# A list scheduler gets a second transfer regime and a table of 215 pairs of priority shifts

## The chip, the cores and the metric

The kernel runs on all eight cores of one Trainium2 chip. Each core computes one of eight batch elements with the same program; the cores exchange nothing. The metric is device time in microseconds (us) of the slowest core. In some runs one die shows a clearly lower TensorE clock and takes longer (the slow state: in one slow run cores 4 to 7 had mean clocks of 0.833 to 0.854, cores 0 to 3 had 0.987 to 0.994); such runs are left out of the medians and ratios below. "Faster" and "slower" mean a ratio more than 2% away from 1.

## The reference, cut to what matters

One layer of a decoder, for 16 meta tokens and 2048 tokens of width 1024:

```python
h = layer_norm(concat([meta, x]))                       # embed
proj = h @ w_in                                         # latents, keys, values, gates
o_mla = causal_block_attention(q_mla, k_mla, v_mla)     # first attention, 8 heads
o_fox = causal_block_attention(fq, fk, fv, cum_logf)    # second attention, 8 heads
merged = g_mla * (o_mla @ w_branch_mla) + g_fox * (o_fox @ w_branch_fox)
h = layer_norm(DN_ALPHA * h + merged @ w_out)           # merge
f = (silu(causal_depthwise_conv(h @ w_up_gate)) * (h @ w_up_val)) @ w_down   # MLP
out = layer_norm(DN_ALPHA * h + f)[16:]
```

## The kernel before

The program is not written in the order in which it runs. A `Recorder` notes some 11,500 items (matmuls, activations, vector operations, transfers) with their dependences, tiles and priorities. Its `order()` then plays a list scheduler through, with a small model of every engine: whenever a modelled engine is free, it takes the ready item of the smallest priority number. The result is a fixed order for each engine, a slot for each tile and, for copies that two engines can do, the engine. On the chip nothing of this is decided again: each engine executes its list strictly in order, and waits on a semaphore where an input is not there. The traces of before show the order: the eight cores ran one and the same sequence of 1,674 instructions on VectorE, 1,362 on ScalarE and 258 on GpSimd, and the six cores whose traces hold every matmul one and the same sequence of 8,316 on TensorE.

```python
class Recorder:
    RES = {"pe": 165.0, "act": 100.0, "dve": 72.0, "pool": 45.0, "sp": 0.0}
    SEM = {"pe": 145.0, "act": 98.0, "dve": 107.0, "pool": 144.0, "sp": 120.0}
    ...
    COLD = 10.0
    RATE = 250.0
    LAND = {"sp": 2000.0, "pool": 2300.0}
    ...
    def _prio(self, e, prio):
        b = prio if prio is not None else self.base.get(e, self.base.get("", 0.0))
        return b * 1e6 + len(self.items)
    ...
    def order(self):
        ...
            if it.dma is not None:
                ks = ["%s%d" % (it.dma, i) for i in range(self.nkeys.get(it.dma, 2))]
                k = min(ks, key=lambda q: keyend.get(q, 0.0))
                st = max(now, keyend.get(k, 0.0))
                bus[0] = max(st + (1450.0 if e == "sp" else 1900.0), bus[0]) + it.bytes / self.RATE + 20.0
                end = bus[0] + self.LAND[e]
                keyend[k] = end
                ...
            else:
                ...
                if e == "pe" and st < 1e3 * self.COLD:
                    dur *= 2
        ...
        self.span = max(freet.values())
```

`self.span` is what I call the scheduler's own **forecast**. A modelled transfer takes 1.45 us to start, then its bytes at 250 bytes per ns on one shared bus, then 2.0 us until its data may be used. *Transposes* (`K.flip`) carry normalised rows and latents into transposed layout, and TensorE multiplies what they deliver. *Loads* bring rows and weight chunks. *Paced casts* copy weights from float32 to bfloat16 in DRAM; they are issued from GpSimd, one at a time, after an activation that the model chose.

```python
        for c in range(8):                       # rank 1: 32 casts for the merge
            for a in (0, 1536):
                for r in range(0, 128, CUT):
                    K.paced(1, "pool", scr_c[c, r:r + CUT, a:a + 1536], d_c[c, r:r + CUT, a:a + 1536], key="pc")
        for j in AHEAD:                          # rank 4: 88 casts for the MLP
            for a in (0, 1024):
                for r in range(0, 128, CUT):
                    K.paced(4, "pool", scr_u[j, r:r + CUT, a:a + 1024], d_u[j, r:r + CUT, a:a + 1024], key="pc")
```

The softmax here doesn't subtract the row's maximum and nothing guards it: scores larger than these inputs give would overflow.

Of the kernel before, what the change touches and what calls it, by code (L numbers as in the profile page):

```python
# [12 lines left out]
class _Op:  # L13
    __slots__ = ("eng", "stream", "pos", "fn", "waits", "clock", "signal", "sigval", "dma")

    def __init__(self, eng, stream, pos, fn, dma):
        self.eng = eng
        self.stream = stream
        self.pos = pos
        self.fn = fn  # L20
        self.waits = []
        self.clock = None
        self.signal = dma
        self.sigval = 0
        self.dma = dma
# [305 lines left out]
class Recorder:  # L331
# [8 lines left out]
    COLD = 10.0  # L340
    RATE = 250.0
    LAND = {"sp": 2000.0, "pool": 2300.0}

    def __init__(self, S):
        self.S = S
        self.items = []
        self.state = {}
        self.nt = 0
        self.base = {}
        self.line = None  # L350
        self.nkeys = {"sp": 16, "pool": 8, "pc": 8, "out": 4, "flip": 8}
        self.pools = []
        self.slow = []

    def slots(self, name, slots, quota=None):
        p = Slots(self, name, slots, quota)
        for s in slots:
            p.keys.update(self.S._keys(s))
        for k in p.keys:
            st = self.state.get(k)  # L360
            if st is not None:
                if st[0] is not None:
                    p.opened.add(st[0])
                p.opened.update(st[1])
        self.pools.append(p)
        return p
# [19 lines left out]
    def _item(self, alts, prio):  # L386
        it = Item()
        it.idx = len(self.items)
        it.alts = alts
        it.tiles = []  # L390
        it.preds = set()
        it.succ = []
        it.dma = None
        it.bytes = 0
        it.done = False
        it.ready = 0.0
        it.end = 0.0
        it.eng = None
        it.prio = prio
        it.key = None  # L400
        it.after = None
        it.tick = False
        it.rank = None
        self.items.append(it)
        return it

# [145 lines left out]

    def _prio(self, e, prio):
        b = prio if prio is not None else self.base.get(e, self.base.get("", 0.0))
        return b * 1e6 + len(self.items)

    def copy(self, out, in_, engs=("act", "dve"), prio=None):
        alts = []
# [31 lines left out]
    def order(self):  # L590
# [17 lines left out]
        bus = [0.0]  # L608
# [55 lines left out]
        def can(it, now):  # L664
            got = {}
            for t in it.tiles:
                if t.slot is None:
                    p = t.pool
                    m = got.get(id(p), 0)
                    ml = got.get((id(p), t.line), 0)  # L670
                    if p.turn.get(t.line, 0) + ml != t.seq:
                        return p, None
                    if p.used.get(t.cls, 0) + m >= p.quota.get(t.cls, 99):
                        return p, None
                    if len(p.free) <= m:
                        return p, None
                    w = p.free[0][0] if m == 0 else sorted(p.free)[m][0]
                    if w > now:
                        return p, w
                    got[id(p)] = m + 1  # L680
                    got[(id(p), t.line)] = ml + 1
            return None, None
# [9 lines left out]
        while ev:  # L692
            now, _, e = heapq.heappop(ev)
            if freet[e] > now + 1e-6:
                continue
            pq = pend[e]
            aq = avail[e]
            while pq and pq[0][0] <= now + 1e-6:
                _, _, it = heapq.heappop(pq)
                if not it.done:  # L700
                    heapq.heappush(aq, (it.prio[e], it.idx, it))
            pick = None
            later = []
            while aq:
                pr, ix, it = heapq.heappop(aq)
                if it.done:
                    continue
                p, when = can(it, now)
                if p is None and it.dma is not None:
                    w = min(keyend.get("%s%d" % (it.dma, i), 0.0) for i in range(self.nkeys.get(it.dma, 2)))  # L710
                    if w > now:
                        p, when = it, w
                if p is not None:
                    if when is None:
                        lst = blocked.setdefault(id(p), [])
                        if it not in lst:
                            lst.append(it)
                    else:
                        later.append((it, when))
                    continue  # L720
                pick = it
                break
            for it, when in later:
                heapq.heappush(pq, (when, it.idx, it))
                wake(when, e)
            if pick is None:
                if pq:
                    wake(max(pq[0][0], now), e) if pq[0][0] > now else None
                continue
            it = pick  # L730
            for t in it.tiles:
                if t.slot is None:
                    p = t.pool
                    _, t.slot = heapq.heappop(p.free)
                    p.used[t.cls] = p.used.get(t.cls, 0) + 1
                    p.turn[t.line] = p.turn.get(t.line, 0) + 1
                    for b in blocked.pop(id(p), []):
                        for (e2, *_r) in b.alts:
                            heapq.heappush(pend[e2], (max(b.ready, now), b.idx, b))
                            wake(max(now, freet[e2]), e2)  # L740
            alt = next(a for a in it.alts if a[0] == e)
            st = now
            dur = alt[4]
            if it.dma is not None:
                ks = ["%s%d" % (it.dma, i) for i in range(self.nkeys.get(it.dma, 2))]
                k = min(ks, key=lambda q: keyend.get(q, 0.0))
                st = max(now, keyend.get(k, 0.0))
                bus[0] = max(st + (1450.0 if e == "sp" else 1900.0), bus[0]) + it.bytes / self.RATE + 20.0
                end = bus[0] + self.LAND[e]
                keyend[k] = end  # L750
                it.key = k
                freet[e] = st + dur
                out.append((it, alt))
                finish(it, "sp", st, end)
            else:
                if e in shape:
                    rw = self.rows(alt[1], alt[2], alt[3])
                    if rw != shape[e]:
                        st = max(st, freet[e] + self.SHIFT)
                        shape[e] = rw  # L760
                if e == "pool" and alt[1] == "tensor_tensor" and port[0] < st < port[1]:
                    dur = max(dur, port[1] + 367.0 - st)
                if e == "dve" and self.twin(alt[1], alt[3]):
                    port = (st, st + dur + 72.0)
                if e == "pe" and st < 1e3 * self.COLD:
                    dur *= 2
                freet[e] = st + dur
                out.append((it, alt))
                finish(it, e, st, st + dur)
                if it.tick and slow and st >= tick and bus[0] <= st + dur + 2100.0 + 1e3 * self.QUIET:  # L770
                    q = next((q for q in slow if q.left == 1), None)
                    if q is not None:
                        slow.remove(q)
                        tick = st + 1e3 * self.GAP
                        q.after = it
                        q.left = 0
                        q.ready = max(q.ready, st + dur + self.RES[e] + self.SEM["pool"])
                        push(q)
            ndone += 1
            wake(freet[e], e)  # L780
# [6 lines left out]
    def replay(self):  # L787
        S = self.S

        def res(v):  # L790
            return v.at(v.t.slot) if isinstance(v, View) else v

        for it, (e, name, args, kw, _d) in self.done:
# [7 lines left out]
            else:  # L801
                it.op = S.op(e, name, *[res(a) for a in args], **kw)

D = 1024
SEQ = 2048
NMETA = 16
# [37 lines left out]
def build_program():  # L844
    nc = bass.Bass("TRN2", target_bir_lowering=False)
    dt_in = lambda n, s: nc.dram_tensor(n, s, F32, kind="ExternalInput").ap()
    xm = dt_in("xm", [L, D])
    lnp = dt_in("lnp", [6, D])
    d_lat = dt_in("w_lat", [128, 8 * 512])
# [16 lines left out]
    d_kt = dt_in("c_kt", [128, NT * 48])  # L866
    out = nc.dram_tensor("out", [SEQ, D], F32, kind="ExternalOutput").ap()
    scr_h2 = nc.dram_tensor("scr_h2", [LP, D], F32, kind="Internal").ap()
    scr_c = nc.dram_tensor("scr_c", [8, 128, 3072], BF16, kind="Internal").ap()
# [858 lines left out]
```

## Time and profile before

| | kernel before |
|---|---|
| time, median of 3 runs | 1097.69 us (1096.46 to 1097.96) |
| spans of the eight cores in the profiled run | 1089.0 to 1095.9 us |
| TensorE busy | 97% of the span |

A core's time divides into stages that the trace marks by the shapes of its matmuls. Medians over the eight cores: the first 65-column matmul (first attention) starts at 70.9 us, the first 64-row matmul (second attention) at 277.3 us, the first 386-column matmul (MLP) at 607.1 us, and the last matmul ends 12.3 us before the end.

The page of the slowest core: the span, the first engine line (busy us and share) and the chain of work that ended last, by engine.

```profile
span 1095.9 us, 25665 instructions; the slowest of 8 cores (1089.0 to 1095.9 us)
...
PE 1061.2 (97%) x8230; PEld 602.7 (55%) x8316; DVE 744.7 (68%) x1674; ACT 619.9 (57%) x1362; POOL 178.9 (16%) x258
...
PE 88%; DMA 3%; issue 2%; ACT 2%; DVE 2%; POOL 1%; SPq 0%; DVEq 0%; POOLq 0%; ACTq 0%
```

TensorE (PE) is the bound, and transfers are hardly on the chain. The waits of TensorE on core 1 from 55 to 165 us, the stretch where transposes feed it (what it waited for: us in total, times, longest):

```profile
PE PS L187 <- ACT SB L187: 2.2, 6, 1.0
PE PS L187 <- DVE SB L187: 1.2, 2, 0.9
PE PS L187 <- DMA SB<-SB: 0.4, 2, 0.2
```

`DMA SB<-SB` is a transpose: the only transfers from on-chip memory to on-chip memory.

Windows of core 0 (busy us of each engine in the stretch, then PEclk, the granted TensorE clock as a share of full speed, then DMA share and GB/s):

```profile
78.00:82.00 4.00, 4.00 (x54) 2.79 (x54) 4.00 (x15) 2.49 (x9) 1.54 (x2) 1.00 0.71 106
82.00:86.00 4.00, 3.96 (x30) 2.06 (x28) 3.79 (x11) 3.88 (x10) 2.53 (x3) 1.00 0.66 154
```

### The profile page before, as it was taken

Reading aid. Unit: us, or ns where it says so; the run is one execution under the profiler, and the core shown is the slowest. Engines: PE = TensorE matmul, PEld = TensorE weight load, DVE = VectorE, ACT = ScalarE, POOL = GpSimd, SP = SyncE. Lnnn points to the kernel's source line nnn. Section 1 sums busy time; section 2 is a strip of 40 time slices with the busy share of each in tenths; the row PEclk is TensorE's granted clock in tenths of the full one; section 3 lists DMA queues with packets and bytes.
Section 4 is the critical chain, followed back from the end, with each engine's and each line's share of the span. In section 5 each row is a group of like instructions: output and inputs, shape, how many; then the busy total and the mean of one; then the engine's idle time right before and its main releaser. Section 6 shows DMA issues by size and latency. Waiting matters only on the chain.

```text
span 1095.9 us, 25665 instructions; the slowest of 8 cores (1089.0 to 1095.9 us)
## 1 busy us (share of the span) xinstructions
PE 1061.2 (97%) x8230; PEld 602.7 (55%) x8316; DVE 744.7 (68%) x1674; ACT 619.9 (57%) x1362; POOL 178.9 (16%) x258
## 2 busy tenths in 40 slices
PE   9999889999999999999999999999999999999995
PEld 6655556667454555565555566554456664444443
DVE  3899866764566676766668887656576765667754
ACT  5789879999778888887873254431034431023300
POOL 5434221121111220302111111101100000110010
PEclk9999999999999999999999999999999999999998
DMA  8858865754677797886989386962242232234301
GB/s 174 206 106 137 146 76 78 137 81 62 156 160 174 123 226 215 148 250 128 226 213 281 98 239 158 257 162 96 99 154 97 97 105 73 112 127 151 107 20 58
DMA packets 86867, 156.54 MB, mean 143 GB/s; under 512 B 39073, under 2 KB 43121, under 8 KB 86737
## 3 DMA queue, kind: packets, MB, share of 16 engines
q1 hardware_dynamic: 70066, 123.78, 38.4%
q0 software_dynamic: 16672, 31.11, 21.3%
q8 instruction: 72, 1.18, 0.5%
q14 instruction: 57, 0.47, 0.2%
HBM read 160.38 MB, written 34.67 MB: 178 GB/s over the span
## 4 chain that ended last, share of the span: by engine, by line
PE 88%; DMA 3%; issue 2%; ACT 2%; DVE 2%; POOL 1%; SPq 0%; DVEq 0%; POOLq 0%; ACTq 0%
PE PS L187 88%; ACT SB L187 2%; DVE SB L187 2%; DMA SB<-SB 2%; DMA SB<-scr_c 1%; POOL SB L187 1%; SPq L190 0%; ACT L187 0%; DVEq L226 0%; POOLq L226 0%; DVEq L245 0%; POOL scr_c L190 0%; POOL SB L190 0%; ACTq L245 0%; SPq L245 0%
## 5 line engine op out<-in xcount | busy, mean ns | idle before, releaser
L187 PE MATMUL PS<-SB 128*128 128x65 bf16 (+11 forms) x8230 | 1061.2, 291 | 22.5 <-DVE SB L187 6.7
L187 PEld LDWEIGHTS PS<-SB 128*128 128x128 bf16 (+2 forms) x8316 | 602.7, 98 | 480.7 <-issue 88.4
L187 ACT ACTIVATE SB<-PS,SB 128x384 bf16<-128x384 f32 (+9 forms) x611 | 315.3, 582 | 250.8 <-PE PS L187 243.9
L187 ACT ACTIVATE SB<-PS 128x384 bf16<-128x384 f32 (+11 forms) x547 | 215.3, 537 | 28.5 <-PE PS L187 24.5
L187 DVE SCALAR_TENSOR_TENSOR SB<-SB 128x1024 f32<-128x1024 f32 (+7 forms) x188 | 177.4, 948 | 14.6 <-POOL SB L187 7.1
L187 ACT ACTIVATE SB<-SB 128x384 f32<-128x384 f32 (+4 forms) x153 | 97.7, 645 | 141.4 <-DVE SB L187 141.1
L187 DVE SCALAR_TENSOR_TENSOR SB<-SB,PS 128x512 f32<-128x512 f32 (+3 forms) x146 | 90.2, 620 | 118.2 <-PE PS L187 93.7
L187 DVE SCALAR_TENSOR_TENSOR SB<-PS,SB 128x384 f32<-128x384 f32 (+1 forms) x220 | 141.0, 642 | 31.9 <-ACT SB L187 23.1
L187 POOL TENSOR_TENSOR SB<-SB 128x1 f32<-128x1 f32 (+1 forms) x67 | 81.8, 1222 | 434.1 <-DVE SB L187 433.6
L187 DVE TENSOR_TENSOR SB<-PS,SB 128x384 bf16<-128x384 f32 (+10 forms) x229 | 108.6, 480 | 61.1 <-ACT SB L187 53.7
L187 DVE TENSOR_TENSOR SB<-SB 128x128 bf16<-128x128 bf16 (+7 forms) x353 | 84.7, 268 | 31.2 <-ACT SB L187 23.7
L190 POOL DMA_DIRECT2D scr_u<-w_u x88 | 44.5, 506 | 266.9 <-ACT SB L187 261.7
L187 DVE CAST SB<-PS 128x512 bf16<-128x512 f32 (+5 forms) x85 | 50.6, 599 | 23.1 <-PE PS L187 18.5
L187 DVE BATCH_NORM_STATS2 SB<-SB 128x6 f32<-128x512 f32 (+1 forms) x85 | 56.9, 675 | 4.6
L187 DVE COPY SB<-SB 32x384 bf16<-32x384 bf16 (+2 forms) x80 | 19.7, 260 | 14.1 <-PE PS L187 12.5
L190 POOL DMA_DIRECT2D scr_c<-w_c x32 | 16.6, 520 | 64.6 <-ACT SB L187 62.7
L187 DVE COPY SB<-PS 128x2 f32<-128x2 f32 (+9 forms) x66 | 19.7, 306 | 8.1 <-PE PS L187 7.7
L190 POOL DMA_DIRECT2D SB<-w_dn x22 | 11.9, 541 | 78.4 <-ACT SB L187 78.4
L187 DVE TENSOR_SCALAR SB<-SB 128x1 f32<-128x1 f32 (+2 forms) x68 | 10.3, 152 | 18.7 <-ACT SB L187 15.9
L187 DVE RECIPROCAL SB<-PS 128x3 f32<-128x3 f32 (+3 forms) x84 | 14.1, 173 | 12.6 <-PE PS L187 11.2
L187 DVE TENSOR_SCALAR SB<-PS,SB 128x128 bf16<-128x128 f32 (+1 forms) x21 | 9.5, 461 | 1.4 <-POOL SB L187 1.0
L187 DVE BATCH_NORM_AGGREGATE SB<-SB 128x2 f32<-128x12 f32 (+2 forms) x43 | 8.6, 203 | 2.4
(20 smaller groups left out, 38.9 us busy)
## 6 DMA issues: line engine op xcount, KB each, us to landing
SB<-scr_u SPq DMA_DIRECT2D x66, 512.0 KB, 3.9
SB<-scr_c SPq DMA_DIRECT2D x80, 384.0 KB, 5.3
SB<-xm SPq DMA_DIRECT2D x31, 512.0 KB, 6.8
scr_u<-w_u POOLq DMA_DIRECT2D x88, 128.0 KB, 4.0
scr_h<-SB SPq DMA_DIRECT2D x16, 512.0 KB, 4.9
SB<-scr_h SPq DMA_DIRECT2D x16, 512.0 KB, 3.5
out<-SB SPq DMA_DIRECT2D x15, 512.0 KB, 2.6
scr_c<-w_c POOLq DMA_DIRECT2D x32, 192.0 KB, 4.2
```

The source lines that it names most:

```text
L187: return self._add(eng, lambda e: getattr(e, name)(*args, **kw), rd, wr)
L190: return self._add(eng, lambda e: e.dma_start(out=out, in_=in_, **kw), [in_], [out], dma_key=key, after=after)
```

## The change

The intent is a better static order, in two parts. The model of transfers gets a second regime: a transfer that starts after 56 us moves 290 bytes per ns and may be used 1.0 us (1.2 us from GpSimd) after its last byte, not 2.0 (2.3). And the program is split into parts, a new one wherever the recorder's stage name changes; each part shifts the priority of its items by a number from a table, one for TensorE and one for the other engines. No arithmetic and no transfer is added or removed.

```diff
+    LATER = 56.0
+    RATE2 = 290.0
+    LAND2 = {"sp": 1000.0, "pool": 1200.0}
...
     def _prio(self, e, prio):
         b = prio if prio is not None else self.base.get(e, self.base.get("", 0.0))
-        return b * 1e6 + len(self.items)
+        k = self.part + (self.line != self.of or self.part < 0)
+        return b * 1e6 + len(self.items) + (RAISED[k][e != "pe"] if k < len(RAISED) else 0)
...
-                bus[0] = max(st + (1450.0 if e == "sp" else 1900.0), bus[0]) + it.bytes / self.RATE + 20.0
-                end = bus[0] + self.LAND[e]
+                late = st >= 1e3 * self.LATER
+                bus[0] = max(st + (1450.0 if e == "sp" else 1900.0), bus[0]) + it.bytes / (self.RATE2 if late else self.RATE) + 20.0
+                end = bus[0] + (self.LAND2 if late else self.LAND)[e]
...
+RAISED = ((-98184, -12242), (90515, -18772), (174186, -48968), ... some 210 more pairs
```

## The prediction

> **What bounds the kernel now.** The page: span 1095.9 us on core 2, TensorE busy 97%. Cores range from 1089.0 to 1095.9 us (view of the cores), clock 0.99. [...] the chain of waits repeats every 10.79 us, 50 matmuls of 512 columns, 216 ns each. All matmuls of core 1 at that rate (my estimate) take 1026 us, 22 of them the 200 filler matmuls at the start. With the table of windows, time minus that work is:
> - 0 to 55 us: 10 us plus most of the filler; first loads bound this (DMA share 0.81).
> - 55 to 164 us: 11 us on core 1, 20 us on core 2. VectorE is 97% busy from 55 to 110 us. On core 2 TensorE waits 5.3 us (waits view, DMA SB<-SB) for DMA transposes that took 6 to 8 us; one slice has clock 0.94.
> - 164 to 274 us: 6 us; ScalarE is 96 to 100% busy (exponentials of the first attention).
> - 274 to 301 us: 5 us, the turn to the second attention.
> - 301 to 575 us: 20 us, but TensorE is 99% "busy": short 65-column matmuls (76 ns each in the groups[...]). Order hardly touches that.
> - 575 to 1069 us: 1 us.[...]
> - tail: 12 us of LayerNorm and store.

> **What the change does.** It adds and removes no operation. It alters the static order: each engine's queue, the slots of the rings, whether ScalarE or VectorE takes a flexible copy, when paced weight casts start. By my reading the 215 parts run to about the end of the merge; the MLP is one late part and stays. Base priorities in the first attention differ by 5,000 a tile and the shifts are tens of thousands: strong reordering. In the second attention bases differ by 100,000 or more: less.

> The modelled transfer after 56 us becomes shorter: a lone 512 KB load 4.3 us, old 5.6; the trace has 3.9. That is better. For a full transpose it becomes worse: 3.2 us, old 4.4, trace median 5.4. An order computed with it can place consumers of transposes too early, and TensorE, in order, waits.

> **Cost.** Addressable is the loss between 27 and 301 us (25 to 35 us); VectorE, then ScalarE are over 95% busy there, so only overlap of the two stages helps. I expect a third: 10 us, plus 2 us from the second attention, less 2 us for transposes later than modelled. All of it is on the critical path: TensorE has no slack afterwards, so the MLP starts earlier by what is gained, unchanged in length. Net 10 us.

> **Prediction: 1087 us, 8 in 10 between 1076 and 1098.** Faster by over 2% (under 1075.7): 0.09. Within 2%: 0.88. Slower by over 2%: 0.03.

> **What would show it.** The first up matmul (386 columns), at 611 us on core 2, comes 6 to 14 us earlier; from there to the end the time stays within 2 us. Loss in 55 to 301 us falls by about 10 us; VectorE and ScalarE totals stay within 10 us. TensorE's waits on DMA SB<-SB remain or grow. Loss in 301 to 575 us stays 17 to 20 us. The tail stays 12 us.

> **What would make it wrong.** The shifts were fitted to a model, and the chip differs: waits on transposes could eat the gain (1095 or more). Or the first 55 us, with the filler, is shortened too, or core 2's loss to clock and transposes vanishes: then 1075.

The chain of waits of which it speaks is that of the MLP. The trace shows the rates themselves: on core 1 of before, after the first 30 us, the median from the start of one matmul to the next is 216 ns for 512 columns, 162 ns for 384 and 29 ns for 65. With these medians for every shape (an estimate, without 8 float32 matmuls for which there is none) the matmuls of core 1 take 1020 us, and the losses by window are 10.4, 10.8 (19.9 on core 2), 6.4, 5.1, 20.6 and 1.6 us, so the list above stands. 10 + 2 - 2 = 10 us, and 1097 less 10 is 1087.

## More of the kernel before

Core 7 from 300 to 600 us, the second attention, hardly waits:

```profile
PE PS L187 <- DVE SB L187: 0.2, 1, 0.2
PE PS L187 <- ACT SB L187: 0.2, 1, 0.2
```

## The result, and the profile after

| | before | after |
|---|---|---|
| time, median of the fast runs | 1097.1 us (4 runs) | 1117.65 us (3 runs, 1116.07 to 1119.36; with the one slow run, 1259.5, the median is 1118.51) |
| ratio of fast runs | | 1.0182 (95% interval 1.0164 to 1.0199) |
| spans of the cores | 1089.0 to 1095.9 us | 1098.9 to 1117.8 us |

A ratio is the mean time of one kernel's fast runs over the mean of the other's fast runs of the same rounds, so it is not quite the ratio of the medians. The change made the kernel 1.8% slower. By the 2% rule that counts as "same", but the interval is far from 1. The page, as shown of before:

```profile
span 1117.8 us, 25623 instructions; the slowest of 8 cores (1098.9 to 1117.8 us)
...
PE 1066.6 (95%) x8230; PEld 601.7 (54%) x8316; DVE 746.3 (67%) x1674; ACT 619.3 (55%) x1362; POOL 177.9 (16%) x258
...
PE 78%; DMA 8%; ACT 4%; issue 4%; DVE 3%; SPq 1%; POOL 1%; DVEq 0%; POOLq 0%; ACTq 0%
```

The work of every engine is the same to within 6 us. What changed is the chain: TensorE falls from 88% to 78% of it and transfers rise from 3% to 8%. Also, the eight cores, which differed by 7 us, now differ by 19 us, although all run the same list. The waits of TensorE on core 1, 55 to 170 us:

```profile
PE PS L187 <- DMA SB<-SB: 9.4, 7, 3.5
PE PS L187 <- ACT SB L187: 2.1, 6, 0.8
PE PS L187 <- DVE SB L187: 1.5, 2, 1.3
PE PS L187 <- issue: 0.2, 1, 0.2
```

The 0.4 us of waiting for transposes have become 9.4 us. Core 1 shows this most clearly; over all eight cores these waits were 0 to 5.3 us before (mean 1.5) and 5.3 to 10.1 after (mean 6.9). The transposes themselves hardly slowed down: those issued between 55 and 166 us took 4.7 us before and 5.2 after, means over the cores. Core 7 from 300 to 600 us, where there was next to no wait before:

```profile
PE PS L187 <- ACT SB L187: 4.9, 4, 3.7
PE PS L187 <- DVE SB L187: 3.6, 3, 2.1
```

On the mean of the cores TensorE waited 0.7 us in this stretch before and 5.4 after. What VectorE (DVE) waited for tells more. In the same window and on the same core it waited for loads of input rows (`xm`); before there is no such line:

```profile
DVE SB L187 <- DMA SB<-xm: 9.9, 6, 3.7
```

These loads did not take longer. Their lines in the DMA view of core 7, the same window, before and then after (the last number is the median from issue to landing):

```profile
SB<-xm SPq DMA_DIRECT2D x16, 512.0 KB, 6.5
SB<-xm SPq DMA_DIRECT2D x13, 512.0 KB, 6.7
```

So the changed order leaves them less time. On the mean of the cores VectorE waited 8.4 us for row loads (before 0.2), and ScalarE 2.0 us for transposes (before 0).

One of TensorE's waits for a transpose, in its timeline on core 0 (start, length, instructions, and in brackets the idle time before them with what ended it):

```profile
73.83 3.71 PE L187 MATMUL PS<-SB 128*128 128x384 bf16 x20
81.86 2.63 PE L187 MATMUL PS<-SB 128*128 128x512 bf16 x16 [4.33 <-DMA SB<-SB]
```

And the windows of core 0 around it, with those of a second wait that ends at 666 us:

```profile
78.00:82.00 4.00, 0.14 (x1) 0.10 (x1) 1.26 (x4) 1.11 (x3) 0.70 (x1) 1.00 0.81 186
82.00:86.00 4.00, 4.00 (x23) 2.53 (x23) 2.45 (x7) 2.47 (x6) 0.00 (x0) 0.57 0.19 71
...
662.00:666.00 4.00, 0.25 (x2) 0.00 (x0) 3.67 (x10) 1.08 (x2) 0.00 (x0) 0.97 0.41 144
666.00:670.00 4.00, 3.55 (x12) 1.91 (x13) 2.98 (x10) 0.52 (x1) 1.62 (x3) 0.50 0.40 47
```

The second wait is named after VectorE, which had itself just waited for a load (`lnp`, the LayerNorm parameters):

```profile
662.22 0.48 DVE L187 SCALAR_TENSOR_TENSOR SB<-SB 128x256 f32<-128x256 f32 x1 [4.22 <-DMA SB<-lnp]
666.45 6.03 PE L187 MATMUL PS<-SB 128*128 128x2 f32 x19 [4.20 <-DVE SB L187]
```

**Where the time went.** The trace lists TensorE's 8,316 matmuls in the order in which the scheduler planned them (the shapes agree one by one), so each has a planned and a real start. The table gives the real minus the planned start, in us, at five planned times. It is the mean over the six cores whose traces hold every matmul in both kernels.

| real minus planned start at planned time | 55 | 160 | 280 | 560 | 700 and end |
|---|---|---|---|---|---|
| before (forecast 1084.4) | 0.9 | 4.1 | 7.3 | 9.1 | -0.5 |
| after (forecast 1074.2) | 1.4 | 12.9 | 16.2 | 24.1 | 27.3 |
| lost by after against before in the stretch | 0.5 | 8.3 | 0.0 | 6.1 | 12.8 |

The forecast promised 10.2 us (1084.4 to 1074.2). The chip fell behind the plan by 27.8 us more than before. The sum, 17.6 us, is what the mean of these cores lost (1091.1 to 1108.4, 17.3 us); the slowest core loses some 4 us more because the cores have spread. There are three losses: in the first attention (55 to 160), in the second (280 to 560), and at the turn from merge to MLP (560 to 700). The third is not a new wait so much as a missing gain: there the kernel *before* ran 9.6 us faster than its own plan, and the changed one does not. New waits are a part of it: between 600 and 700 us TensorE waited 3.3 us on the mean core, before 0.3.

### The profile page after: what moved, and what is told of

Its sections match the earlier page's. It is cut to its first block, busy times and chain, and to the rows that moved or that the text cites. A ratio compares the mean times of both kernels' runs of the same rounds, so it can differ in the third digit from the quotient of the medians.

```text
span 1117.8 us, 25623 instructions; the slowest of 8 cores (1098.9 to 1117.8 us)
## 1 busy us (share of the span) xinstructions
PE 1066.6 (95%) x8230; PEld 601.7 (54%) x8316; DVE 746.3 (67%) x1674; ACT 619.3 (55%) x1362; POOL 177.9 (16%) x258
## 4 chain that ended last, share of the span: by engine, by line
PE 78%; DMA 8%; ACT 4%; issue 4%; DVE 3%; SPq 1%; POOL 1%; DVEq 0%; POOLq 0%; ACTq 0%
PE PS L187 78%; ACT SB L187 4%; DMA SB<-xm 3%; DMA SB<-SB 3%; DVE SB L187 3%; DMA SB<-lnp 1%; SPq L190 1%; DMA SB<-scr_c 1%; POOL SB L187 0%; DMA scr_h<-SB 0%; POOL SB L190 0%; DVEq L226 0%; DVEq L245 0%; POOLq L226 0%; ACTq L245 0%
## 5 line engine op out<-in xcount | busy, mean ns | idle before, releaser
L187 PE MATMUL PS<-SB 128*128 128x65 bf16 (+9 forms) x8230 | 1066.6, 291 | 39.2 <-DVE SB L187 19.6
L187 PEld LDWEIGHTS PS<-SB 128*128 128x128 bf16 (+1 forms) x8316 | 601.7, 98 | 503.7 <-issue 112.0
L187 ACT ACTIVATE SB<-PS,SB 128x384 bf16<-128x384 f32 (+8 forms) x615 | 317.0, 580 | 266.4 <-PE PS L187 260.2
L187 ACT ACTIVATE SB<-PS 128x384 bf16<-128x384 f32 (+12 forms) x543 | 213.5, 560 | 29.5 <-PE PS L187 26.0
L187 DVE TENSOR_TENSOR SB<-PS,SB 128x384 bf16<-128x384 f32 (+9 forms) x229 | 108.2, 480 | 64.5 <-ACT SB L187 57.9
L187 DVE TENSOR_TENSOR SB<-SB 128x128 bf16<-128x128 bf16 (+8 forms) x353 | 84.3, 268 | 33.4 <-ACT SB L187 27.8
L187 DVE CAST SB<-PS 128x384 bf16<-128x384 f32 (+5 forms) x85 | 50.1, 590 | 18.3 <-PE PS L187 16.7
L187 DVE TENSOR_SCALAR SB<-SB 128x1 f32<-128x1 f32 (+2 forms) x68 | 10.5, 154 | 18.8 <-ACT SB L187 16.0
L187 DVE TENSOR_SCALAR SB<-PS,SB 128x384 bf16<-128x384 f32 (+1 forms) x17 | 8.4, 504 | 2.4 <-POOL SB L187 1.9
```

Source lines behind the costliest of these rows:

```text
L187: return self._add(eng, lambda e: getattr(e, name)(*args, **kw), rd, wr)
```

## The experiments

**The theories.** *A: lost margin.* The new regime gives a transfer about its median real time. On core 1 the transposes of after took 4.9 us in the median and the model said 4.7, but one in ten came 2.1 us or more later than planned. For the kernel before the model said 6.2 us, the trace 4.8, and one in ten came 0.1 us late or more. In a fixed order an early transfer gains nothing and a late one stops an engine that executes in order. *B: the table.* It is a bad or brittle order by itself, whatever the transfer model. All experiments give correct results except the two that say otherwise. "Over" is the median time of the fast runs minus the scheduler's own forecast: 13 us for before, 43 us for after (the expectations say 44, from the median with the slow run).

| experiment | forecast | median | over | ratio to before | half clock |
|---|---|---|---|---|---|
| e1: new model, no shifts | 1088.7 | 1122.02 | 33 | 1.0201 | 8.5 us |
| e2: shifts, old model | 1106.7 | 1125.90 | 19 | 1.0218 | 23.9 us |
| e3: after, casts later | 1074.2 (as after) | 1128.21 | | 1.0257 | 20.5 us |
| e4: before, casts later | 1084.4 (as before) | 1107.12 | | 1.0062 | 8.5 us |
| e5: fresh table for the new model | 1071.4 | 1113.88 | 43 | 1.0146 | 8.1 us |
| e6: fresh table for the old model | 1074.7 | 1101.65 | 27 | 1.0040 | 2.6 us |
| e7: old model, 1 us more margin | 1093.8 | 1104.99 | 11 | 1.0064 | 6.0 us |
| e8: new model, transposes 2 us later | 1089.9 | 1116.63 | 27 | 1.0178 | 7.7 us |
| e9: after, few casts (wrong result) | 1074.2 (as after) | 1109.79 | | 1.0071 | 6.0 us |
| e10: before, few casts (wrong result) | 1084.4 (as before) | 1093.04 | | 0.9923 | 0.0 us |
| e11: table judged by late transfers | 1082.7 | 1100.72 | 18 | 0.9992 | 2.1 us |
| e12: after, waits filled | 1074.2 (as after) | 1114.25 | | 1.0160 | 3.8 us |

Half clock is the time at clock 0.5 on the mean core. The first four ran on one chip, where before took 1100.41 us, the next four on another (1098.00), then e9 to e11 (1101.55), then e12 (1097.64); so compare ratios. By the 2% rule e3 is slower, e1, e2 and e8 are unclear, the others count as same; every 95% interval but that of e11 leaves out 1. The diffs below are shortened.

### The two parts alone: e1 and e2

```diff
 # e1
-        return b * 1e6 + len(self.items) + (RAISED[k][e != "pe"] if k < len(RAISED) else 0)
+        return b * 1e6 + len(self.items) + 0
 # e2
-    LATER = 56.0
+    LATER = 1e9
```

> One part of the change alone: the two-regime transfer model, with all priority shifts zero. The scheduler's own forecast is 1088.7 us (1084.4 for the kernel before, 1074.2 for the changed one). Theory A (the new transfer model took away a hidden margin: it gives a transfer its median time, so about half of them come later than the static order assumes, and an in-order engine then waits): the chip is 20 us or more over the forecast, 1108 to 1135 us, although no shift is in it. Theory B (the table of shifts is the fault, a bad order on any chip): 1096 to 1102 us, near the kernel before.

> The other part alone: the shifts, with the old transfer model. The scheduler's own forecast is 1106.7 us, so the shifts do not suit that model. The kernel before runs 13 us over its forecast, the changed one 44 us over. Theory A: with the old, late transfers in the model this order keeps its forecast as the kernel before does: 6 to 16 us over it, 1112 to 1123 us. Theory B: the shifted order is brittle by itself and again runs 30 us or more over its forecast, above 1136 us.

The new model alone, without one shift, costs 2.0% and runs 33 us over its forecast, as theory A said. But lateness is not all of it. Under the new transfer times the order *before* would end at 1078.6 us (see the replays below), and the order of e1, made for these times, at 1088.7: even with no transfer late, the scheduler found an order 10 us worse. That leaves some 12 of the 22 us for late transfers and half clock. The table alone costs 2.2%, but 22 us of that the scheduler foresaw (1106.7 against 1084.4): the table was made for the other model. It ran 19 us over its forecast, a little above the 16 that A allowed and far from B's 30. The trace shows where the rest is: on core 1 TensorE was at half clock for one stretch of 20.5 us, from 590 us on.

```profile
590.00:610.00 20.00, 15.28 (x112) 7.63 (x110) 8.70 (x24) 11.03 (x24) 2.44 (x4) 0.51 0.86 215
```

The clock was 0.51 in that window, which costs up to 8 us (an estimate: half of TensorE's 15.3 busy us), and all eight cores had 20 us or more at half clock. Neither part helps alone, and together they are as slow as each.

### Moving the casts away from the transposes: e3 and e4

```diff
+    def later(self, since, gap):
+        casts = [x for x in self.done if x[0].rank is not None and x[0].rank[0] in (1, 4)]
+        ...   # the order stays; each cast moves behind an activation that starts after `since`
+        K.later(166.0, 2.6)
         K.replay()
```

> The changed kernel with its order frozen on every engine; only the paced weight casts (copies from memory to memory on the GpSimd queue) start after 166 us of the model's time instead of 70. [...] Theory A (TensorE waits there because transposes land later than assumed): transposes of that stretch land sooner, the 9.4 us that TensorE of core 1 waits for DMA SB<-SB fall under 4 us, and the kernel gains 4 to 10 us: 1108 to 1114 us. Theory B (the order itself, not late transfers): gain under 2 us.

> The same move of the casts in the kernel before, its order frozen. Its TensorE waits 0.4 us on core 1 and 5.3 us on core 2 for transposes there. Theory A: the order before has margin, so it gains less than the changed kernel does: 0 to 4 us, 1093 to 1097 us. If both gain the same, contention is a cost of its own and does not explain the difference between the two kernels.

Both times missed. In the stretch itself the transposes did land sooner: the mean of the 16 on core 1 fell from 5.4 to 4.1 us (over all cores from 5.2 to 4.5), and core 1's waits on them from 9.4 to 3.5 us, as expected. So transposes were faster with the casts out of the way; by what mechanism is not shown. But core 2's waits rose from 5.4 to 7.1 us, the mean over the cores fell only from 6.9 to 4.5, and the stage hardly got shorter (the second attention began at 280 us in place of 281, medians). So the casts are at most a part of what makes TensorE wait for transposes in this order; as the theory of the first stage they fell.

The two kernels then lost time elsewhere: the second attention took 315.7 us in place of 299.5 (e3) and 306.8 in place of 293.0 (e4). I had moved casts into a stretch where the loads for the merge run, and loads took longer there. On core 1 of e4 the mean load of a merge weight took 7.9 us (5.1 before) and a row load issued after 166 us 8.3 (6.0). This says something the experiment was not made for: with its order frozen, the kernel before, too, pays 14 us in that stage once transfers land later than its plan.

### Is it this table? e5 and e6

A random search started from a table of zeros. Each try changed 1 to 60 entries by random amounts (standard deviation 5,000 to 40,000) and was kept if the forecast did not rise; some 5,600 tries each. One search used the new transfer model, the other the old one, and the order was made by the same model.

```diff
 # e5
-RAISED = ((-98184, -12242), (90515, -18772), (174186, -48968), ...
+RAISED = ((-13567, 8299), (-48227, -51950), (65836, -83322), ...
 # e6: another table, and
-    LATER = 56.0
+    LATER = 1e9
```

> A fresh table of 214 pairs, found here by a random search of some 5,600 tries that minimised the scheduler's own forecast under the new two-regime model, in place of the table of the change. Forecast 1071.4 us. Theory A (an order tuned to median transfer times has no margin): 30 us or more over its forecast, 1101 to 1118 us, slower than the kernel before. Theory B (the table of the change is one unlucky order; the new model is sound): a fresh table keeps most of its gain, 1084 to 1094 us.

> The same search, same length, same mutations, but under the old, late transfer model, which also makes the order. Forecast 1074.7 us (1084.4 without a table). Theory A: the late transfers leave margin, so it runs 8 to 16 us over its forecast as the kernel before does: 1083 to 1091 us, faster than the kernel before by 6 to 14 us. Rival (a table fitted to any model of transfers is brittle on the chip): 1097 us or more.

e5 came out as A expected: 43 us over its forecast and 1.5% slower than before. The table of the change was not an unlucky one. e6 went against A: 27 us over its forecast, 0.4% slower than before, where A said 8 to 16 us over and faster. So fitting is a second cause. Under each model the excess rose by some 10 to 14 us with a fitted table: from 33 to 43 (new model), from 13 to 27 (old model). Still, the two together are the cleanest test of the transfer model: the same search, forecasts 3 us apart, and on the same chip the table of the late model came out 12 us faster. The real-minus-planned curve of e6 shows how: it stands at 15.0 us at planned time 560, after 9.1 for before, and does not come back at the turn to the MLP (16.6 at the end, before -0.5). The old model expected waits there that the chip does not have. The search removed those modelled waits, which the forecast counted as a gain and the chip could not. (A replay agrees: under the new transfer times e6's order ends only 3.5 us before that of the kernel before, not 9.7.)

### More margin, and margin for transposes alone: e7 and e8

```diff
 # e7, on the kernel before
-    LAND = {"sp": 2000.0, "pool": 2300.0}
+    LAND = {"sp": 3000.0, "pool": 3300.0}
 # e8, on e1
-                end = bus[0] + (self.LAND2 if late else self.LAND)[e]
+                end = bus[0] + (self.LAND2 if late else self.LAND)[e] + (2000.0 if late and it.dma == "flip" else 0.0)
```

> The kernel before with 1 us more of landing time in its model (3.0 and 3.3 us in place of 2.0 and 2.3), no shifts: more margin. Forecast 1093.8 us. Theory A: the excess of the chip over the forecast falls with margin, 33 us for the new model, 13 us for the old one, now under 9 us: 1096 to 1103 us. If margin is not what sets the excess, it stays at 13 us or more: 1107 us or above.

> The new transfer model without shifts (as in the first experiment, which ran 33 us over its forecast), but transposes alone land 2 us later in it. Forecast 1089.9 us. If too early transposes are the main cause: the excess falls to 8 to 18 us, 1098 to 1108 us. If the margin of all transfers matters: it stays above 24 us, 1114 us or more.

e7: the excess fell only from 13 to 11 us, between the two expectations, and the time rose with the forecast. More margin than the kernel before has is not worth it. e8: the excess stays at 27 us, as expected if all transfers matter. Yet transposes did what the first stage needed: between planned times 55 and 160 the chip fell behind by 4.3 us (e1: 9.7; before: 3.2), TensorE's waits on transposes fell to 1.4 us on the mean core (e1: 6.3; before: 1.5), and from the start of the first attention to the end of the rotary stage (the last 72-column matmul) it took 73.2 us in place of 79.8 (medians). After that stretch e8 loses as e1 does. So in the first attention the modelled time of transposes is the main cause of these waits; later it must be something else.

### The traffic taken away: e9 and e10

```diff
         K.order()
+        for it, alt in K.done:
+            if it.rank is not None and it.rank[0] in (1, 4) and <not chunk 0>:
+                continue                       # 8 of 120 casts stay
+            elif <a load of scr_c[c] or scr_u[j]>:
+                alt[3]["in_"] = <the same piece of chunk 0>
+            keep.append((it, alt))
+        K.done = keep
         K.replay()
```

> The changed kernel with its order frozen, but only the first of eight and the first of 22 weight chunks are cast (8 of 120 casts remain), and every later load of a weight chunk reads that one: same loads, same arithmetic, WRONG RESULT on purpose. It takes the cast traffic away from the transfers that the engines wait for, without moving it to another stretch as the third experiment did. Theory A (late transfers, and half-clock windows after the waits, make the difference between the kernels): the changed order comes close to its forecast[...]: 1090 to 1103 us, 15 us or more under its 1118, with TensorE's idle time on the mean core under 17 us (23 with casts). Theory B (the order itself): a gain under 8 us.

> The same cut of the casts in the kernel before, order frozen, wrong result on purpose. Theory A: its order had the margin already, so it gains 0 to 8 us (1089 to 1097), and the changed kernel is then within 10 us of it, in place of 20. Theory B: both gain alike and the 20 us stay.

Against before on the same chip, after without casts is 0.7% slower (1.8% with them), and before without casts is 0.8% faster. By the slowest core the gap between the kernels thus falls only from 1.8% to 1.5%; on the mean of the eight cores it falls from 16 us (1092.1 and 1108.4) to 10.5 us (1088.4 and 1098.9). That is less than A expected (cut from its text is a figure for the cast traffic, an estimate of mine that no run shows). By stage, however, the answer is sharp:

| stage, median of the cores | before | e10 | after | e9 |
|---|---|---|---|---|
| start to second attention | 277.3 | 275.0 | 281.0 | 281.0 |
| second attention | 293.0 | 293.0 | 299.5 (294.5 to 303.9) | 293.7 (293.2 to 294.2) |

In the second attention the changed order loses 6 us to the traffic of the casts, and the cores' spread goes with it; the order before loses nothing to the same traffic. That is what margin means. Core 7 of e9, 300 to 600 us, against the lines shown of after:

```profile
PE PS L187 <- ACT SB L187: 1.2, 3, 0.6
PE PS L187 <- DVE SB L187: 0.2, 1, 0.2
```

The waits named ACT and DVE there (8.5 us in after) are down to 1.4 us (mean of the cores 5.4 to 1.4). VectorE's waits for row loads on this core fell with them:

```profile
DVE SB L187 <- DMA SB<-xm: 1.5, 2, 0.8
```

These engines, too, execute in order (one sequence on all cores, as said of the kernel before) and pass a late load on. GpSimd also had 112 casts fewer to issue, a rival for the gain; but VectorE's waits for GpSimd are 1.1 us in both, so the gain is the loads'. (Stage times of before and after come from one chip, those of e9 and e10 from another, on which before was 0.4% slower.) Up to the second attention e9 gains nothing at all (281.0 us with and without the casts): it still loses 10.4 us between planned 55 and 160 and core 1 waits 7.1 us for transposes (mean of the cores 5.7, after 6.9), with 4 of the 18 casts of that stretch left: again, casts are not its main cause, and e8 showed what is.

### A table chosen with lateness in the judgement: e11

The search of e6 again (2,400 tries), but each try's fixed order was replayed with eight draws of lateness, sampled from the traces of these runs by kind of transfer, and with a half-rate window after a mostly idle one, as the clock records show them (last section); the score is the mean and the worst draw.

> A table searched as before under the old transfer model, but every try is judged by replaying its fixed order with eight draws of transfer lateness, sampled from the traces of these runs, and a half-rate TensorE clock after a mostly idle window; the score weighs the mean and the worst draw. Forecast 1082.7 us; the replays say 8 to 9 us less than for the kernel before. If late transfers and the half clock are what matters: faster than the kernel before by 3 to 10 us, 1087 to 1095 us. If any table is brittle on the chip for other reasons (the engines' own times): 1098 us or more.

A tie: ratio 0.9992 (0.9974 to 1.0010), neither the gain that the replays promised nor the loss of e6. The curve stands at 11.5 us at planned 560 and comes back to 6.9 at the end. Judging by late transfers took away the damage of fitting, not more. It is the best of the tables tried; no version here beats the kernel before.

### Filling the waits: e12

```diff
         K.order()
+        # before 8 matmuls that waited on most cores: 6 to 20 matmuls of 256 columns into the
+        # same bank, with constant operands; the waiting matmul then overwrites it
```

> The changed kernel, order frozen, with 86 extra matmuls of 256 columns (about 110 ns each, 9.5 us in all) put in front of eight matmuls at which TensorE was seen to wait in the trace of most cores; they write the bank that the waiting matmul then overwrites, so the result stays right. They take TensorE's time only where the wait is shorter than they are. The waits themselves are not shortened. If half-clock windows after the waits are a real part of the loss: time at half clock on the mean core falls from 7.2 us to under 3.5 us and the time falls by 1 to 6 us against the changed kernel, ratio to the kernel before 1.012 to 1.017. If the half clock costs nothing: the ratio stays at 1.018 or rises to 1.026, by what the extra matmuls take where the wait was shorter.

The expectation says 86 matmuls; the program and the trace have 88. Half clock fell from 7.2 to 3.8 us on the mean core, less than expected. The ratio is 1.0160 (1.0134 to 1.0186), inside the range for "half clock is real", but its interval holds 1.0182 as well. So 88 extra matmuls cost nothing net, which shows that TensorE was waiting at those points. How many of the microseconds are the half clock's own stays unsettled by this run; what rests on the trace is the clock record, the doubled spacing of the matmuls and the bound of 3.5 us given above.

### Replays of the fixed orders

One check used no chip time. I replayed each kernel's fixed order with the engines as modelled but with each transfer taking what the trace of one core shows. The order before then ends at 1077.9 to 1082.1 us, depending on the core, which is *less* than its forecast of 1084.4; with the new regime's times it ends at 1078.6. The order after ends at 1083.5 to 1095.8, *more* than its forecast of 1074.2, and differently for each core. Two things follow. The new order's gain under fair transfer times was never 10 us but 4.5 (1078.6 to 1074.1): the rest was the old model's pessimism, which the chip had never paid. And real lateness costs the new order 14.8 us on the mean of six cores (1088.9 against 1074.1), the old one 1.0 us (1079.6 against 1078.6). With 4 us for an average of 8.0 us at half clock on these cores (an estimate: half of it), the sum is -4.5 + 13.8 + 4 = 13 us of the 17.3 us that they lost; the remaining 4 us are not attributed.

A second program puts the order before at 1079.5 us with the new regime's times and, over all eight cores, at 1077.4 to 1082.5 with traced ones; the order after at 1074.1, and at 1081.0 to 1095.8 (1083.5 to 1095.8 without core 4, which is not one of the six). So take these figures as good to about 1 us. It also shows the margin of the two fresh tables: with traced times e5 ends 17 us over its forecast (1088.7, mean of the cores) and e6 5 us over (1080.1).

## Why the prediction was wrong

- **Right: the bound and what stays.** TensorE in order is the bound; the MLP from its first to its last up matmul took 300.5 us before and 300.3 after (medians; 5 to 7 us more on the three cores that had a half-clock window at about 666 us); the tail is 12 us; VectorE's total moved from 744.7 to 746.3 us and ScalarE's from 619.9 to 619.3.
- **Right in kind, wrong in size: "less 2 us for transposes later than modelled".** This is the term that was mis-sized. In the first attention the changed order lost 8.3 us against before; e8 shows, without the table, that the modelled time of transposes makes most of such a loss (9.7 to 4.3 us, with 3.2 for before). I had the numbers (model 3.2 us for a full tile, trace median 5.4) and named waits on transposes as the risk, but priced them as a small correction.
- **Wrong: "I expect a third: 10 us", "plus 2 us from the second attention".** Three things were missed. First, the forecast's gain was partly air: 5.8 of 10.2 us were waits of the old model that the chip did not have (replay), and at the turn to the MLP the old plan was beaten by 9.6 us. Second, the second attention lost 6 us instead of gaining 2: the order had no room for the traffic of the casts (e9 and e10), and VectorE waited 8.4 us for row loads. Third, the half clock after a wait was not in the sum at all (up to 3.5 us on the mean core, an estimate).
- **Wrong: "That is better", of the loads.** I took a transfer model nearer to the trace's median for a better one. The row loads of the second attention show why it is not: the plan of the changed kernel gives them 6.6 us and they took 6.6 (medians over the cores, 300 to 600 us), so that 52% came later than planned, and VectorE waited for them. The plan of the kernel before gives them 9.5 us, they took 6.5, and 4% came late. e1 is the answer: the model alone costs 2.0%, some 10 us of it by a worse order and the rest, as far as is known, by transfers that came later than planned. The old model's extra landing time worked as slack: the table fitted under it (e6) ran 12 us faster than the one fitted under the new model (e5).
- **Wrong sign, so the marks failed.** The first up matmul on core 2 comes at 627 us, not before 605. Waits on transposes: 5.3 to 5.4 us on the slowest core, which looks unchanged, but 0.4 to 9.4 us on core 1 and 1.5 to 6.9 on the mean core. Looking at the slowest core alone hides it, since core 2 had the longest such waits of all cores before. The worst case that I wrote, "1095 or more", named the right risk, but the result lies 20 us above the upper end of my range, 1098.
- **Still open:** which loads make the lost gain at the turn to the MLP (12.8 us against plan); why the scheduler finds a worse order under the new model (e1); the 4 us not attributed; the exact price of the half clock below its bound (e12).

## What to carry to other kernels

A static order is executed by engines that wait in order, so a transfer time in its model should be a late one, not the typical one: fast transfers gain nothing, slow ones stop everything behind them (in the second attention of after 52% of the row loads came later than planned, and VectorE waited 8.4 us for them). A search that minimises a model's own forecast finds the model's errors first; before trusting its gain, replay the old order under the new model (here it left 4.5 of 10 us), replay the new order under late times (under the old model's the changed order ends at 1119.5, the order before at 1084.4, by the second replay program), and judge candidates with measured lateness on all cores. And a wait on TensorE of 2 to 4 us can cost more than its length, because a half-clock window may follow it (in after such windows followed waits of 1.98 us, which ended at 487 us on core 5, and of 4.33 us, which ended at 82 us on core 0; 384-column matmuls then started 320 ns apart in place of 162).

## What else the traces show of the clock and of landing times

- In the fourteen profiles here, 177 half-clock stretches began after the start-up; in the 3.413 us before them TensorE had been busy for 37% in the median, and for less than half in 144 of them (in before and after alone 33% in the median, and less than half in all 17). So a wait well under 3.413 us also came before such a stretch: 1.98 us on core 5 of after, with TensorE busy for 42% of the 3.413 us before the stretch. The share does not decide alone: on the grid on which these stretches lie, every window with TensorE busy for under 30% was followed by one, but 20 windows with 30 to 47% were not (in before and after alone: 8 of 8 under 30%, and 3 with 42 to 44% that were not).
- Most profiles, all of fast runs, hold no clock record between 0.5 and 1 (before and after: none). In those of e9 to e11 there are stretches of 15.1 us at 0.81, up to three on a core, on cores 0 to 3 only, between 582 and 726 us. The mean clocks fit: in e10, which has no half-clock stretch after the start-up, cores 0 to 3 have 0.988 to 0.995 and cores 4 to 7 0.995 to 0.998. What sets this clock is not shown. The slow runs, in which a core's mean clock fell to 0.82 to 0.96, have no kept trace.
- The landing time of a transfer spreads widely: 47 transposes of before took 2.3 to 8.9 us on core 2, and on core 1 of after a tenth of them came over 2 us later than a model close to the median; that tail, not the median, is what TensorE waited for in the first attention.
